# A branch for rare rows moved ahead of the last scatter, in a hard-max attention kernel

## The chip, the cores and the metric

One core of a Trainium2 chip. The time is device microseconds of the execution; before the change the median of three runs is 488.95 us (488.84 to 489.34).

## The reference

```python
def setup_inputs():
    B, Sq, Sk, D = 4, 4096, 4096, 128
    # q, k, v: standard normal, float32

def reference(q, k, v):
    logits = np.matmul(q, k.transpose(0, 2, 1))
    best = np.argmax(logits, axis=-1)
    b_idx = np.arange(q.shape[0])[:, None]
    return v[b_idx, best, :].astype(np.float32)
```

For each of 4 x 4096 query rows the kernel finds the key with the largest product and copies that key's row of v. Nothing is averaged, so a wrong winner is a wrong row.

## The kernel before, in words

The work is 128 query tiles of 128 rows (T = 128, NQT = 32 per batch). Keys are grouped by four. For each tile TensorE computes a rough fp16 score of every group, ScalarE and VectorE fold them into a packed word of score and group number, and a top-eight (line 230) leaves the best groups of every row in `TOP`. For the best group, POOL gathers the differences of its four keys (`kg`, line 247), VectorE computes the dot products and picks the winner (`pick`), and POOL gathers the winner's row of v into `vr` (line 304). Every eight tiles (four at the end) SP stores `vr` to the output (line 308). The gathers of `vr` wait in a list, `late_q`; `take_late(n)` issues the next n of them.

The order of instructions on each engine is the order in which the Python code emits them: the whole body stands in a manual schedule (`man`).

Some rows are too close to call from the rough scores. They are flagged and computed once more in fp32. The first half of the tiles is done in `flag_segment`, spread over the main loop; the second half in `flags_first` and `flags_last`, behind the main loop. `flags_last` gives up to 128 flagged rows one partition each, gathers their record, their query, and three candidate groups of keys (`FR`, `FQ`, `FK`, by the helper `get`, line 494), computes the exact products (`exact`, line 533), gathers the winners' rows of v into `FV`, and scatters `FV` to the output by the row numbers `row` (line 525). A row number beyond the output is dropped by the scatter's bounds check, which is how unused partitions are left out. Between these steps `late(n)` issues gathers of `vr`; `late(1 << 20)` ahead of the scatter issues all that are left, with their stores. As the scatter overwrites rows that the stores of `vr` have written, it must come behind them.

`HARD` counts what this way cannot settle: flags beyond 128 in a half, more than eight flagged tiles in one partition, rows whose fourth group is close too. It is the same number in all partitions, and is last changed at line 520, well ahead of the exact products. If it is above zero, `all_rows` (lines 562 to 584) computes every row again from the records in DRAM: line 564 copies the count to an integer `hi`, line 565 loads it into a register of each of the five engines' queues, line 567 branches, and the body is four loops over tiles, with stores from SP. On the inputs used here the count is zero and the branch is not taken.

When the branch is skipped, each engine's queue passes through a skip side, whose steps are put down to line 567: they bring the semaphores to where the body would have left them. On SP these are eight waits with an increment; on POOL four waits and one instruction INC_SWDGE_SEM. The end of the program is put down to line 764: SP's last waits, a DRAIN on every engine, a barrier, and the clearing of semaphores.

In the kernel before, the manual schedule ends behind `flags_last`, and `all_rows` comes after it: the scatter is issued first, then the branch.

Of the kernel before, what the change touches and what calls it, by code (L numbers as in the profile page):

```python
# [7 lines left out]
FP32 = mybir.dt.float32  # L8
FP16 = mybir.dt.float16
BF16 = mybir.dt.bfloat16  # L10
U32 = mybir.dt.uint32
# [4 lines left out]
OP = mybir.AluOpType  # L16
AF = mybir.ActivationFunctionType
IOA = bass.IndirectOffsetOnAxis
# [9 lines left out]
def kernel(ctx, tc, q, k, v, out):  # L28
    nc = tc.nc
    B, Sq, D = q.shape  # L30
    Sk = k.shape[1]
    P = 128
# [7 lines left out]
    out_flat = out.rearrange("b s d -> (b s) d")  # L40
# [7 lines left out]
    fp = ctx.enter_context(tc.tile_pool(name="flag", bufs=1))  # L48
# [82 lines left out]
    HARD = cp.tile([P, 1], FP32, tag="HARD")  # L131
# [6 lines left out]
    FV = cp.tile([P, P], FP32, tag="FV")  # L138
# [309 lines left out]
    def flags_last(t0, t1, win_last, late):  # L448
# [25 lines left out]
        for s in range(8):  # L474
# [13 lines left out]
                                op0=OP.logical_shift_right)  # L488
        nc.vector.scalar_tensor_tensor(out=rw[:, 1:2], in0=tb[:, 1:2], scalar=float(Sq - NQT), in1=rw[:, 1:2], op0=OP.mult, op1=OP.add)
        row = fp.tile([P, 1], U32, tag="row", name="row_e")  # L490
        nc.vector.scalar_tensor_tensor(out=row, in0=rw[:, 1:2], scalar=-1.0, in1=rw[:, 0:1], op0=OP.add, op1=OP.add)

        def get(dst, src, idx, hi):
# [9 lines left out]
                                op0=OP.logical_shift_right, op1=OP.logical_shift_left)  # L503
# [15 lines left out]
        for a in (hd[:, 0:1], hd[:, 1:2], tot[:, 2:3]):  # L519
# [2 lines left out]
        win = whole(exact(FK, FQ, gb, 3, "fe"))  # L522
        get(FV, v_flat, win, B * Sk)
        late(1 << 20)
        nc.gpsimd.indirect_dma_start(out=out_flat, out_offset=IOA(ap=row, axis=0), in_=FV, in_offset=None,  # L525
                                     bounds_check=P * T - 1, oob_is_err=False)

    def exact(kk, qq, grp, R, name):
        d = fp.tile([P, R, 4], FP32, tag=f"xd{R}", name=f"xd_{name}")
        for r in range(R):  # L530
            for f in range(4):
                pr = fp.tile([P, P], FP32, tag="xp", name=f"xp_{name}_{r}_{f}", bufs=2)
                nc.vector.tensor_tensor_reduce(out=pr, in0=kk[:, r, f * P:(f + 1) * P], in1=qq, scale=1.0, scalar=0.0,
                                               op0=OP.mult, op1=OP.add, accum_out=d[:, r, f:f + 1])
                yield "dve", 0.2
        ix = fp.tile([P, R, 4], FP32, tag=f"xi{R}", name=f"xi_{name}")
        nc.vector.scalar_tensor_tensor(out=ix, in0=grp.unsqueeze(2).to_broadcast([P, R, 4]), scalar=4.0,
                                       in1=iota4.unsqueeze(1).to_broadcast([P, R, 4]), op0=OP.mult, op1=OP.add)
        yield "dve", 0.17
        mx = fp.tile([P, 1], FP32, tag="xm", name=f"xm_{name}")  # L540
        nc.vector.tensor_reduce(out=mx, in_=d.rearrange("p r f -> p (r f)"), axis=AX_X, op=OP.max)
        yield "dve", 0.17
        lt = fp.tile([P, R * 4], FP32, tag=f"xl{R}", name=f"xl_{name}")
        nc.vector.tensor_scalar(out=lt, in0=d.rearrange("p r f -> p (r f)"), scalar1=mx, scalar2=float(1 << 20),
                                op0=OP.is_lt, op1=OP.mult)
        yield "dve", 0.17
        nc.vector.tensor_tensor(out=lt, in0=lt, in1=ix.rearrange("p r f -> p (r f)"), op=OP.add)
        yield "dve", 0.17
        win = fp.tile([P, 1], U32, tag="xw", name=f"xw_{name}")
        nc.vector.tensor_reduce(out=win, in_=lt, axis=AX_X, op=OP.min)  # L550
        yield "dve", 0.17
        return win


    def whole(g):
        while True:
            try:
                next(g)
            except StopIteration as s:
                return s.value  # L560

    def all_rows():
        hi = fp.tile([1, 1], mybir.dt.int32, tag="hi")
        nc.vector.tensor_copy(out=hi, in_=HARD[0:1, :])
        left = nc.values_load(hi[0:1, 0:1], min_val=0, max_val=1 << 24,  # L565
                              skip_runtime_bounds_check_because="a count of rows, summed in fp32")
        with tc.If(left > 0):
            for b in range(B):
                with tc.For_i(0, NQT, 1) as t:
                    w8 = fp.tile([P, 8], U32, tag="aw", name=f"aw_{b}")  # L570
                    nc.sync.dma_start(out=w8, in_=rec.rearrange("(p b t) w -> b p t w", b=B, t=NQT)[b][:, bass.ds(t, 1), :].rearrange("p o w -> p (o w)"))
                    qn = fp.tile([P, P], FP32, tag="aq", name=f"aq_{b}")
                    nc.sync.dma_start(out=qn, in_=q[b].rearrange("(p t) d -> p t d", p=P)[:, bass.ds(t, 1), :].rearrange("p o d -> p (o d)"))
                    g8 = fp.tile([P, 8], U32, tag="ag", name=f"ag_{b}")
                    nc.vector.tensor_scalar(out=g8, in0=w8, scalar1=NG - 1, scalar2=(NG - 1) | (b * NG),
                                            op0=OP.bitwise_and, op1=OP.bitwise_xor)
                    kk = fp.tile([P, 8, 512], FP32, tag="ak", name=f"ak_{b}")
                    for r in range(8):
                        nc.gpsimd.indirect_dma_start(out=kk[:, r, :], out_offset=None, in_=k4,
                                                     in_offset=IOA(ap=g8[:, r:r + 1], axis=0))  # L580
                    win = whole(exact(kk, qn, g8, 8, f"a{b}"))
                    vv = fp.tile([P, P], FP32, tag="av", name=f"av_{b}")
                    nc.gpsimd.indirect_dma_start(out=vv, out_offset=None, in_=v_flat, in_offset=IOA(ap=win, axis=0))
                    nc.sync.dma_start(out=out[b].rearrange("(p t) d -> p t d", p=P)[:, bass.ds(t, 1), :].rearrange("p o d -> p (o d)"), in_=vv)
# [141 lines left out]
    for p in [s for s in live if s["kind"] == "pick"]:  # L726
# [6 lines left out]
        if last:  # L733
            flags_first(T // 2, T)
        drain([p], "cnt" if last else None)
    flags_last(T // 2, T, lambda: drain([p]), take_late)
    man.__exit__(None, None, None)
    all_rows()


# [28 lines left out]
```

## Time and profile before

| what | value |
|---|---|
| median of the runs | 488.95 us |
| the profiled execution, whole | 488.95 us |
| its span, first to last instruction | 487.0 us |
| PE busy | 389.1 us, 80% |
| VectorE (DVE) busy | 421.0 us, 86% |
| ScalarE (ACT) busy | 395.5 us, 81% |
| GpSimd (POOL) busy | 302.3 us, 62% |
| last exact product's winner (`xw`, line 550) ends | 462.3 us |
| last gather of `vr` starts | 466.35 us |
| last scatter (line 525) starts | 471.86 us |

Times inside a profile are microseconds from the span's start. A name with a q (POOLq, SPq, DVEq) is the engine's instruction queue, which runs ahead of the engine and handles waits, branches, register loads and the issue of transfers; these steps are not counted as busy. A transfer's "landing" is when its semaphore says that the data are there. Durations in the answers for one line are nanoseconds.

### The profile page before, as it was taken

The page shows a single profiled execution, that of the slowest core. Times are in us where ns is not written, and L with a number is a line of the kernel's source. Part 1 is how long each engine was busy: PE and PEld are TensorE (multiplying, and loading weights), DVE is VectorE, ACT ScalarE, POOL GpSimd, SP SyncE. Part 2 cuts the span into 40 slices and gives each one's busy share as a digit, 9 for nine tenths or more (in the row PEclk, how much of TensorE's full clock was granted, in tenths as well). Part 3 has the DMA queues.
Part 4 walks back from the last instruction along what each step waited for, and adds up shares of the span by engine and source line. Part 5 has one row for each costly group of instructions (what it writes and reads, how often), then busy time and mean ns, then how long its engine had stood idle before and what let it go on. Part 6 is the DMA issues. An engine that isn't in the chain of part 4 may idle for free. (4 is left out here: it accounts for less than half of the span.)

```text
span 487.0 us, 6530 instructions
## 1 busy us (share of the span) xinstructions
PE 389.1 (80%) x1960; PEld 176.1 (36%) x1960; DVE 421.0 (86%) x849; ACT 395.5 (81%) x498; POOL 302.3 (62%) x345
## 2 busy tenths in 40 slices
PE   6798899999997999999997889999999888901000
PEld 3344444444443444444443334444433333301000
DVE  4278999999999799999998899999999999997400
ACT  1999999999997899999996889999999878900000
POOL 9025445666788676566887565576776567667730
PEclk9999999999999899999998999999999999965555
DMA  8514452131546451313456431313241311323320
GB/s 137 134 26 69 94 110 62 55 100 55 123 93 169 105 132 56 100 55 105 95 100 159 105 99 53 96 56 105 75 131 53 100 49 57 108 61 121 97 74 0
DMA packets 24552, 43.48 MB, mean 89 GB/s; under 512 B 7976, under 2 KB 16171, under 8 KB 24512
## 3 DMA queue, kind: packets, MB, share of 16 engines
q0 software_dynamic: 18464, 30.97, 28.5%
q1 hardware_dynamic: 6048, 12.06, 6.8%
q8 instruction: 15, 0.25, 0.2%
q14 instruction: 25, 0.20, 0.1%
HBM read 39.59 MB, written 12.19 MB: 106 GB/s over the span
## 5 line engine op out<-in xcount | busy, mean ns | idle before, releaser
L201 ACT ACTIVATE A<-pd 128x1024 f16<-128x1024 f32 x256 | 262.8, 1033 | 12.1 <-PE pd L192 11.6
L247 POOL DMA_INDIRECT kg<-k,cand x128 | 125.4, 979 | 121.1 <-DVE p L266 43.9
L227 DVE TENSOR_TENSOR W<-psn,E 128x1024 int16<-128x1024 f32 x128 | 166.5, 1301 | 24.1 <-ACT E L214 11.2
L192 PE MATMUL psn<-kT,qT 128*128 128x512 f16 x512 | 153.0, 380 | 18.0 <-ACT A L201 12.1
L192 PE MATMUL pd<-kT,qT 128*128 128x512 f16 x512 | 153.5, 381 | 11.1 <-ACT A L201 9.6
L230 DVE MAX8 TOP<-W 128x8 f32<-128x1024 f32 x128 | 156.2, 1220 | 0.0
L211 PE MATMUL psn<-A,identh 128*128 128x512 f16 x512 | 153.0, 380 | 0.0
L192 PEld LDWEIGHTS <-qT 128*128 128x128 f16 x1024 | 96.4, 98 | 150.0 <-issue 71.3
L304 POOL DMA_INDIRECT vr<-in_v_dram,win x128 | 124.1, 970 | 39.3 <-issue 35.6
L214 ACT ACTIVATE E<-psn 128x1024 int16<-128x1024 f32 x128 | 131.1, 1024 | 3.5 <-PE psn L211 3.5
L211 PEld LDWEIGHTS <-identh 128*128 128x128 f16 x512 | 49.9, 97 | 61.6 <-issue 1.4
L262 DVE TENSOR_TENSOR prod<-kg,natq 128x768 f16<-128x768 f16 x64 | 35.0, 549 | 0.0
L174 ACT ACTIVATE qT<-uq 128x256 f16<-128x256 f32 x60 | 23.8, 396 | 5.4 <-PE uq L172 5.4
L266 DVE TENSOR_TENSOR p<-prod 128x384 f16<-128x384 f16 x64 | 22.3, 351 | 0.0
L172 PE MATMUL uq<-identh,natq 128*128 128x128 f16 x120 | 16.6, 220 | 6.9 <-DMA natq<-in_q_dram 5.5
L271 DVE TENSOR_REDUCE D<-p 128x6 f32<-128x192 f16 x64 | 21.5, 339 | 0.0
L167 ACT ACTIVATE kT<-uk 128x256 f16<-128x256 f32 x48 | 19.0, 396 | 1.1 <-PE uk L164 1.1
L172 PEld LDWEIGHTS <-natq 128*128 128x128 f16 x120 | 11.3, 99 | 20.3 <-DMA natq<-in_q_dram 8.2
L163 PE MATMUL uk<-identh,natk 128*128 128x128 f16 x96 | 15.8, 219 | 0.6 <-ACT A L201 0.6
L63 POOL DMA_DIRECT2D natk<-in_k_dram x26 | 15.7, 602 | 0.9 <-POOLq L753 0.8
L269 DVE TENSOR_TENSOR p<-p 128x192 f16<-128x192 f16 x64 | 15.7, 248 | 0.0
L66 POOL DMA_DIRECT2D natq<-in_q_dram x26 | 15.5, 596 | 0.0
(149 smaller groups left out, 160.6 us busy)
## 6 DMA issues: line engine op xcount, KB each, us to landing
out_dram<-vr SPq DMA_DIRECT2D x14, 512.0 KB, 3.0
k<-kd SPq DMA_DIRECT2D x8, 384.0 KB, 3.3
natk<-in_k_dram POOLq DMA_DIRECT2D x24, 128.0 KB, 3.6
natq<-in_q_dram POOLq DMA_DIRECT2D x24, 128.0 KB, 3.1
kg<-k,cand POOLq DMA_INDIRECT x128, 2.7
vr<-in_v_dram,win POOLq DMA_INDIRECT x128, 2.5
natk<-in_k_dram POOLq DMA_DIRECT2D x2, 512.0 KB, 6.1
out_dram<-vr SPq DMA_DIRECT2D x4, 256.0 KB, 2.0
```

Of the source, the lines that this page charges most:

```text
L172: nc.tensor.matmul(out=ps[:, i * P:(i + 1) * P], lhsT=natq[b % 2][:, g * 2 + i, :], rhs=identh, start=True, stop=True)
L174: nc.scalar.activation(out=qT[b % 2][:, g * 256:(g + 1) * 256], in_=ps, func=AF.Copy, scale=QSCALE)
L192: nc.tensor.matmul(out=ps[:, n * 512:(n + 1) * 512], lhsT=qT[b % 2][:, qt * P:(qt + 1) * P], rhs=kT[b % 2][:, u * 1024 + n * 512:u * 1024 ...
L201: nc.scalar.activation(out=A, in_=ps, func=AF.Abs)
L211: nc.tensor.matmul(out=ps[:, n * 512:(n + 1) * 512], lhsT=identh, rhs=A[:, n * 512:(n + 1) * 512], start=False, stop=True)
L214: nc.scalar.activation(out=E, in_=ps, func=AF.Relu)
L227: nc.vector.tensor_tensor(out=W_t[t % NW].bitcast(I16)[:, 1::2], in0=ps, in1=E, op=OP.max)
L230: nc.vector.max(out=TOP[:, t, :], in_=W_t[t % NW].bitcast(FP32))
L247: near_q.append(lambda j=j: nc.gpsimd.indirect_dma_start(out=kg[:, j].rearrange("p f d -> p (f d)"), out_offset=None, in_=k16[t0 // NQT], ...
L262: nc.vector.tensor_tensor(out=prod, in0=kg, in1=natq[b % 2][:, x - b * NQT:x - b * NQT + m, :].unsqueeze(2).to_broadcast([P, m, 3, P]), op ...
L266: nc.vector.tensor_tensor(out=p1, in0=prod[:, :, :, 0:64], in1=prod[:, :, :, 64:128], op=OP.add)
L304: late_q.append(lambda j=j: nc.gpsimd.indirect_dma_start(out=vr[:, j, :], out_offset=None, in_=v_flat, in_offset=IOA(ap=win[:, j:j + 1], a ...
```

## The change

The call of `all_rows` moves from behind the manual schedule into `flags_last`, ahead of the last scatter. Since the general path would now write its rows before the scatter and not after it, the scatter must write nothing when that path has run: a mask `ok` is 2^20 in every partition when `HARD` is above a half, else zero, and is added to the row numbers, so that all of them fall beyond the output and are dropped. These are two VectorE operations on 128x1 numbers. The exact products themselves are computed as before.

```diff
         win = whole(exact(FK, FQ, gb, 3, "fe"))
         get(FV, v_flat, win, B * Sk)
         late(1 << 20)
-        nc.gpsimd.indirect_dma_start(out=out_flat, out_offset=IOA(ap=row, axis=0), in_=FV, in_offset=None,
+        ok = fp.tile([P, 1], FP32, tag="ok", name="ok_e")
+        nc.vector.tensor_scalar(out=ok, in0=HARD, scalar1=0.5, scalar2=float(1 << 20), op0=OP.is_gt, op1=OP.mult)
+        rowk = fp.tile([P, 1], U32, tag="rowk", name="rowk_e")
+        nc.vector.tensor_tensor(out=rowk, in0=row, in1=ok, op=OP.add)
+        all_rows()
+        nc.gpsimd.indirect_dma_start(out=out_flat, out_offset=IOA(ap=rowk, axis=0), in_=FV, in_offset=None,
                                      bounds_check=P * T - 1, oob_is_err=False)
...
     flags_last(T // 2, T, lambda: drain([p]), take_late)
     man.__exit__(None, None, None)
-    all_rows()
```

## The prediction

> **What bounds the kernel now.** The edit sits behind the last matrix product, so I read the end of the span first. The page's second part cuts the 487.0 us into 40 slices of 12.2 us:
>
> ```profile
> DVE  4278999999999799999998899999999999997400
> ...
> POOL 9025445666788676566887565576776567667730
> ```
>
> In the last slice no engine is busy, and in the one before it POOL has three tenths. The page's chain counts busy work and ends with POOL's last scatter, so it stops at 472.9, some 14 us before the span does. The chain of waits from 462 on:
>
> ```profile
> 466.35 0.94 POOL vr L304
> 467.30 3.66 issue
> 470.95 0.04 POOLq L525
> ...
> 472.15 0.72 POOL out_dram L525
> ```
>
> The 3.66 us called "issue" is POOL idle until its queue reaches L525 at 470.95. POOL's waits put its idle time there down to SP (total, times, longest), and SP's own timeline shows the store concerned:
>
> ```profile
> POOL out_dram L525 <- SPq L567: 4.6, 1, 4.6
> ```
>
> ```profile
> 468.88 0.33 SPq L308 DMA_DIRECT2D out_dram<-vr  x1
> ```
>
> The last store of normal rows goes out at 468.88 and lands 2.0 us later, at 470.9. The scatter writes the same output and must come behind it. Then the answer for line 567 (the branch; columns: queue, kind, count, ns min/median/max, first and last start):
>
> ```profile
> L567 SPq EVENT_SEMAPHORE  x8: 17/17/17, 470.3 to 471.3; - x8
> L567 POOLq EVENT_SEMAPHORE  x4: 17/43/1634, 472.7 to 473.0; - x4
> ...
> L567 DVEq COMPARE_BRANCH  x1: 72/72/72, 462.7 to 462.7; - x1
> L567 DVEq EVENT_SEMAPHORE  x1: 21/21/21, 465.7 to 465.7; - x1
> ...
> L567 POOLq COMPARE_BRANCH  x1: 53/53/53, 472.2 to 472.2; - x1
> L567 POOLq INC_SWDGE_SEM  x1: 2390/2390/2390, 474.6 to 474.6; - x1
> ```
>
> The body of the branch has no row in the trace: it is skipped, and these are the steps of the skip side. POOL's queue waits there until every transfer it has issued has landed; the 1.63 us wait ends at 474.6, which is the scatter's start plus its 2.7 us to landing (471.86 + 2.7). Only then comes INC_SWDGE_SEM, 2.39 us. And the kernel's last line, 764:
>
> ```profile
> L764 SPq EVENT_SEMAPHORE  x14: 17/28/28, 477.0 to 486.9; - x14
> L764 POOLq DRAIN  x3: 46/103/9056, 477.1 to 486.7; - x3
> ```
>
> One POOL DRAIN of 9.06 us begins at 477.1, straight behind INC_SWDGE_SEM, and ends at 486.1; 0.9 us of closing steps follow. So the end is a chain on POOL's queue alone: store landed 470.9, scatter 471.86, landed 474.6, INC to 477.0, DRAIN to 486.1, close at 487.0.
>
> **The change part by part.** The profiled execution took 488.95 us, which is the median of the three runs too; 1.95 us of it lies outside the span (488.95 - 487.0).
>
> The two new VectorE operations (ok, rowk) and the copy to hi, which in the trace ran at 454.4 and now stands behind them, are three 128x1 or 1x1 operations of 0.14 to 0.16 us. They run behind xw, which ends at 462.3, and are done by about 462.9. ScalarE and TensorE then load hi some 8 us later than now, and nothing else is queued on them. POOL's queue stood at L525 from 462.4 on, so it is held back by 0.5 us and still has 6 us to go until the last vr gather's landing. Cost nothing; if that cover were gone, 0.5 us.
>
> The branch moves ahead of the scatter. On POOL's queue that brings, in order: the load of hi (0.51 us), the compare, the four waits, INC_SWDGE_SEM, and then the scatter with its own waits. The load and compare are over near 463.6. A branch can cost more than its row: on VectorE 2.9 us pass from the compare at 462.7 to the next instruction at 465.7, on POOL 0.5 us (472.2 to 472.7), on SP 0.5 us (its compare at 469.8, next step at 470.3). I take POOL's own 0.5; with VectorE's 2.9 the queue would be ready at 466.5, still before the gathers have landed. [...]
>
> Now the waits of the skip side end with the last vr gather instead of the scatter: issue 466.35 plus 2.5 to landing (the median of that line's issues) is 468.85. INC_SWDGE_SEM runs from there to 471.24. Most of that lies beside the wait for the store's landing at 470.9, which the scatter has to sit out anyway. The scatter must also come behind SP's eight skip steps, the last at 471.3, because SP's stores in the body write the same output; that is a new wait, and nothing is queued behind the scatter but the end. Its four queue waits, at the 0.09 us between the two short ones of now, bring 471.65; from the queue's last wait row (ended 471.08) to the scatter's start (471.86) it was 0.78 us, so it starts at 472.43, 0.57 later than now, and ends at 473.44 with its 1.01 us.
>
> What is removed is everything now standing between the scatter's end and the DRAIN: 472.87 to 477.1, 4.2 us, that is 1.7 us of landing and 2.4 us of INC. SP's final waits still need the scatter's landing (472.43 + 2.7 = 475.1), but SP is done long before the DRAIN. DRAIN at its 9.06 us from 473.44 ends at 482.5; 0.9 to close gives a span of 483.4, and 1.95 outside it gives **485.3 us**, 3.6 below the median (0.57 lost ahead of the scatter, 4.2 gained behind it).
>
> The trace does not say what the 9.06 us are made of, nor when the DRAIN's clock starts behind a transfer in flight. The nearest rows are the opening DRAIN of POOL (0.17 us, nothing issued yet) and this one. If it takes its length from the scatter's dispatch, 1.2 us before the scatter's end, the time is 484.1; from its landing (475.1), 487.0. At the far end below, a DRAIN that only waits for the landing and adds 0.17 gives 475.3 + 0.9 + 1.95 = 478.2. At the far end above, it is paid in full twice (below). I take 9.06 from the scatter's end, as it is the same instruction behind the same list of some 320 POOL transfers. Half a microsecond either way for the queue's steps makes the likeliest case's own range 484.1 to 486.2.
>
> The main part of the kernel, up to 440, keeps its order on every engine: zero.
>
> **The rivals.** *DRAIN counts from the landing*: 487.0, faster by 1.9. For it: today it starts with everything landed, so the trace never shows it overlapping a transfer.
>
> *The 9.06 us belong to INC_SWDGE_SEM*, and DRAIN merely waits for its tail. The trace has the two back to back and cannot part them. Then the POOL engine is held from 471.24 to 480.3, the scatter starts at 481.4 and lands at 484.1, a short DRAIN of 0.17 and the close give 485.2, with 1.95 it is 487.1. Against it: SP's final waits, on the semaphores that INC raises, were released at 477.0, so INC had done its visible work by its own end.
>
> *Slower: the idle time is paid twice.* If POOL has to come to rest behind the skip side before it may issue again, and once more at the end, both at 9.06, the scatter starts at 481.4, ends at 482.4, DRAIN ends at 491.5 and the time is 494.3, 5.4 above. It decides once the second stretch is over 4.6 us (482.4 + 4.6 + 0.9 + 1.95 = 489.9). Against it: ScalarE, TensorE and VectorE run from their compare straight to line 764 without a barrier at line 567, so the skip side has no common stop, and no DRAIN row stands at line 567.
>
> *Nothing moves*: the end is tied to something that the order on POOL's queue doesn't shift, or the scatter is still issued in its old place: 488.95. Against it: the whole chain from 471.9 to 486.1 is consecutive on that one queue.
>
> *Much faster*: the DRAIN shrinks, since it no longer follows INC directly: 478.2 to 483.6.
>
> **How the numbers follow.** Likeliest case 0.62; DRAIN from the landing 0.13; INC's tail 0.07; paid twice 0.09; nothing moves 0.05; much faster 0.04. A measurement of this kernel tells about 0.2% (1.0 us) from no change. Faster: 0.62 + 0.13 + 0.07 + 0.04 = 0.86; same 0.05; slower 0.09. The range holds the likeliest case with the two that end at 487, 0.82 together, with half a microsecond of queue steps on either end: 483.6 to 487.6.
>
> **What would show it.** In the profile after, INC_SWDGE_SEM should start near 468.9 and end near 471.2, ahead of the scatter; the scatter should start at 472.1 to 472.9; DRAIN should start within 1.2 us of the scatter's end and last about 9 us; the span should be about 483.4. A gap of several us between INC_SWDGE_SEM and the scatter speaks for INC's tail or a double stop; a DRAIN of over 10 us for counting from the landing. A DRAIN row of several us at line 567, or a span above 488, makes the prediction wrong.

## The result, and the profile after

The changed kernel takes 484.63 us (median of four runs, 484.01 to 485.53) against 489.06 for the kernel before: the ratio is 0.991, with a 95% interval from 0.9891 to 0.993. The forecast was 485.3, in a range of 483.6 to 487.6. The profiled execution took 485.16 us with a span of 483.1, 3.9 below that of before.

The end of the span, first POOL's own work (start, duration, engine, line, operation):

```profile
465.99 0.95 POOL L304 DMA_INDIRECT vr<-in_v_dram,win  x1 [0.30 <-DMA vr<-in_v_dram,win]
472.18 1.01 POOL L530 DMA_INDIRECT out_dram<-FV,rowk_e  x1 [5.24 <-issue]
```

Then the answer for line 572, where the branch now stands:

```profile
L572 SPq EVENT_SEMAPHORE  x8: 17/17/17, 470.0 to 471.0; - x8
L572 POOLq EVENT_SEMAPHORE  x4: 17/43/43, 463.6 to 467.2; - x4
...
L572 POOLq COMPARE_BRANCH  x1: 53/53/53, 463.1 to 463.1; - x1
...
L572 DVEq COMPARE_BRANCH  x1: 72/72/72, 463.2 to 463.2; - x1
L572 DVEq EVENT_SEMAPHORE  x1: 21/21/21, 466.2 to 466.2; - x1
L572 POOLq INC_SWDGE_SEM  x1: 2370/2370/2370, 468.6 to 468.6; - x1
```

and for line 768, the end of the program:

```profile
L768 SPq EVENT_SEMAPHORE  x14: 17/28/3199, 471.1 to 483.0; - x14
...
L768 POOLq DRAIN  x3: 46/109/10311, 471.9 to 482.8; - x3
```

INC_SWDGE_SEM has changed sides: it runs from 468.6 to 470.9, behind the landing of the last gather and ahead of the scatter. The scatter starts 0.3 us later than before, at 472.18, and ends at 473.2. The long DRAIN row begins when POOL's queue reaches it, at 471.9, even ahead of the scatter; it ends at 482.3, which is 9.07 us behind the scatter's end. Nothing stands between the two any more. The scatter lands at 474.4 (SP's 3.2 us wait in line 768 ends there) while the DRAIN runs.

### The profile page after: what moved, and what is told of

It is laid out like the page before. It is cut to its first block, busy times and chain, and to the rows that moved or that the text cites. A ratio compares the mean times of both kernels' runs of the same rounds, so it can differ in the third digit from the quotient of the medians.

```text
span 483.1 us, 6533 instructions
## 1 busy us (share of the span) xinstructions
PE 389.5 (81%) x1960; PEld 176.5 (37%) x1960; DVE 419.8 (87%) x851; ACT 395.4 (82%) x498; POOL 303.4 (63%) x345
## 4 chain that ended last, share of the span: by engine, by line
DVE 39%; ACT 21%; issue 17%; PE 11%; DMA 7%; POOL 3%; POOLq 0%; DVEq 0%; ACTq 0%
ACT A L201 16%; DVE W L227 16%; DVE TOP L230 7%; DMA natq<-in_q_dram 4%; ACT E L214 4%; DVE prod L262 4%; PE psn L192 4%; PE pd L192 3%; PE psn L211 3%; DVE p L266 2%; DVE D L271 2%; DMA vr<-in_v_dram,win 2%; POOL vr L304 1%; DVE cand L241 1%; DVE p L269 1%
## 5 line engine op out<-in xcount | busy, mean ns | idle before, releaser
L201 ACT ACTIVATE A<-pd 128x1024 f16<-128x1024 f32 x256 | 262.5, 1031 | 11.5 <-PE pd L192 11.0
L172 PE MATMUL uq<-identh,natq 128*128 128x128 f16 x120 | 16.6, 220 | 7.3 <-DMA natq<-in_q_dram 5.8
```

Source lines behind the costliest of these rows:

```text
L172: nc.tensor.matmul(out=ps[:, i * P:(i + 1) * P], lhsT=natq[b % 2][:, g * 2 + i, :], rhs=identh, start=True, stop=True)
L201: nc.scalar.activation(out=A, in_=ps, func=AF.Abs)
```

## The experiments

The loop's length differs a little from run to run, so the table gives, besides the ratio to the kernel before of the same set, the length of the end alone: from the start of the last gather of v (line 304) to the end of the span, all from the profiled executions.

| kernel | ratio to before (95%) | scatter after last gather, us | INC_SWDGE_SEM, us | DRAIN's end after the scatter's end, us | length of the end, us |
|---|---|---|---|---|---|
| before | 1 | 5.5 | 2.39 | 13.3 | 20.6 |
| mask_only | 1.0017 (0.9999 to 1.0035) | 5.6 | 2.39 | 13.2 | 20.6 |
| after | 0.991 (0.9891 to 0.993) | 6.2 | 2.37 | 9.07 | 17.1 |
| after_again | 0.9906 (0.9878 to 0.9934) | 6.3 | 2.37 | 9.07 | 17.2 |
| move_only | 0.992 (0.9868 to 0.9971) | 6.1 | 2.37 | 9.07 | 17.0 |
| no_branch | 0.988 (0.9852 to 0.9907) | 5.5 | none | 9.06 | 16.3 |
| branch_early | 1.0016 (0.9993 to 1.0039) | 5.6 | 2.31 | 9.07 | 16.6 |
| extra_12 | 0.9776 (0.9753 to 0.9799) | 6.0 | 0.50 | 1.99 | 9.9 |
| extra_30 | 0.9801 (0.9773 to 0.9829) | 6.3 | 0.86 | 2.86 | 11.0 |
| before_12 | 0.9816 (0.9749 to 0.9882) | 5.6 | 0.52 | 4.2 | 11.6 |

move_only and before_12 ran together on a chip on which the kernel before takes 519.8 us; their loops are some 23 to 33 us longer (by the start of the last top-eight), so only the ratio and the end are used of them. In branch_early INC_SWDGE_SEM runs ahead of the last gather, so its cost does not show in the last column.

**The parts of the change.** The mask without the move, and the move without the mask, both as edits of the changed kernel:

```diff
 # mask_only: the branch stays behind the scatter
         nc.vector.tensor_tensor(out=rowk, in0=row, in1=ok, op=OP.add)
-        all_rows()
...
     man.__exit__(None, None, None)
+    all_rows()
 # move_only
-        nc.gpsimd.indirect_dma_start(out=out_flat, out_offset=IOA(ap=rowk, axis=0), in_=FV, in_offset=None,
+        nc.gpsimd.indirect_dma_start(out=out_flat, out_offset=IOA(ap=row, axis=0), in_=FV, in_offset=None,
```

> The kernel before with the mask alone: ok and rowk are computed and the scatter uses rowk, but the branch stays behind it. Theory: the two operations lie on VectorE behind xw, 9 us ahead of the scatter, and cost nothing: 489, as before, with the scatter near 471.9 and INC_SWDGE_SEM behind its landing. Rival, the gain is the mask's, or the operations hold POOL: 1 us or more from 489.

> The changed kernel with row in place of rowk in the scatter: the branch is moved, the mask is left out of use (if the general path were taken, the scatter would overwrite its rows). Theory: all of the gain is the move's: 484.5 to 485.3, the scatter at 472.2, the closing DRAIN 9.07 us from its end. Rival, part of it comes with the mask: over 486.

mask_only is 489.29 us, ratio 1.0017, and its end is that of before to 0.1 us. move_only's ratio is 0.992 and its end that of after to 0.1 us. The count `HARD` is zero in all of these runs, so neither the mask's other value nor the general path ran in any of them. The gain is the move's alone; the absolute times expected of move_only were not met, as the chip was another.

**The changed kernel once more**, as the measure of its set:

> The changed kernel as it is, so that the others of this set stand beside it on the same chip. Expected 484 to 485.5 us, against 489 before.

It is 484.96 us.

**Whose are the 9 us?** The kernel before, without the general path:

```diff
     man.__exit__(None, None, None)
-    all_rows()
```

> The kernel before without the general path: no load of hi, no branch, no skip side (rows that need it would stay as the scatter leaves them). It parts INC_SWDGE_SEM from the closing DRAIN. Theory A, the DRAIN's 9.07 us are its own and count from the scatter's end: scatter at 471.9 to 472.9 as before, DRAIN ends at 482.0, span 482.8, time 484.7, the same as the changed kernel, because there INC_SWDGE_SEM lies beside the wait for the last store. Theory B, the 9 us are INC_SWDGE_SEM's tail: the DRAIN ends soon after the scatter's landing at 474.6, span about 475.5, time about 477.5.

It takes 484.41 us. The scatter in the answer for its line, and the DRAIN in the answer for the last line:

```profile
L525 POOL DMA_INDIRECT out_dram<-FV,row_e x1: 1019/1019/1019, 472.1 to 472.1; - x1
```

```profile
L763 POOLq DRAIN  x3: 46/97/10310, 471.9 to 482.7; - x3
```

With no INC_SWDGE_SEM near it the DRAIN still ends 9.06 us behind the scatter's end (471.9 + 10.31 = 482.2, less 472.1 + 1.02). Theory A holds, and the tail of INC_SWDGE_SEM is no explanation. The run also prices what is left of the branch in the changed kernel: the scatter comes 5.5 us after the last gather here and 6.2 there, so SP's and POOL's skip steps still cost 0.7 us.

**Is the skip side free only under its cover?** The branch ahead of the last three gathers:

```diff
-        late(1 << 20)
         ok = fp.tile([P, 1], FP32, tag="ok", name="ok_e")
...
         all_rows()
+        late(1 << 20)
         nc.gpsimd.indirect_dma_start(out=out_flat, out_offset=IOA(ap=rowk, axis=0), in_=FV, in_offset=None,
```

> The changed kernel with the branch one step earlier still: ahead of the last three gathers of v, and so without the cover of the wait for the last store (the general path's rows of the last tiles would be overwritten, were it taken). Theory A, the skip side is free only because it lies beside that wait: INC_SWDGE_SEM then runs from the landing of FV, about 465.0, to 467.4, the three gathers follow at 1.25 us each and land at about 473, the last store lands at 475.1, the scatter starts at 476.0, the DRAIN ends at 486.1, time 488.9, some 4 us above the changed kernel. Rival, the skip side costs nothing wherever it stands: 485.

The median is 490.05 us and the profiled execution 488.93. POOL's timeline:

```profile
461.29 1.00 POOL L494 DMA_INDIRECT FV<-in_v_dram,xw_fe  x1 [1.17 <-DVE hi L569]
467.81 0.94 POOL L304 DMA_INDIRECT vr<-in_v_dram,win  x1 [5.52 <-DMA FK<-in_k_dram,gb_e]
...
475.93 1.02 POOL L530 DMA_INDIRECT out_dram<-FV,rowk_e  x1 [4.68 <-issue]
```

POOL stands still for 5.5 us between FV and the next gather: the wait for the landing, then INC_SWDGE_SEM (464.8 to 467.1), then the restart. The scatter starts at 475.93, where 476.0 was expected. One step too early costs all that the change gains.

**What does the closing DRAIN count?** A DRAIN was put into POOL's order in the loop, behind iterations 30, 60, 90 and 118 (drain_4), behind 64 (drain_1), behind every eighth (drain_8), and, in drain_qe, behind iterations without loads, with one more ahead of the branch:

```diff
         step(it)
         issue(it)
+        if it in (30, 60, 90, 118):        # drain_1: (64,)   drain_8: it % 8 == 6
+            nc.gpsimd.drain()
...
+        nc.gpsimd.drain()                  # drain_qe only
         all_rows()
```

> The changed kernel with a DRAIN put into POOL's order behind iterations 30, 60, 90 and 118 of the main loop. It asks what the closing DRAIN's length counts. Theory C, it counts the transfers issued on POOL since the last DRAIN (about 322 now, so 28 ns each): some 50 are left after iteration 118, the closing DRAIN takes about 1.4 us from the scatter's end or ends with the scatter's landing, and the span is 6 to 8 us shorter at its end; each DRAIN in the loop holds POOL for some 2.5 us of landing and 2 us of its own, of which VectorE may wait 0 to 3 us; time 478 to 484. Theory D, it has a fixed length, or one that goes with the whole program: it stays at 9 us, the loop pays as well, time 485 to 520.

drain_4 takes 492.65 us, ratio 1.0073 (1.0047 to 1.0098): the time falls in theory D's range, but not with theory D's DRAIN. Its closing DRAIN and scatter:

```profile
L770 POOLq DRAIN  x3: 46/109/5139, 484.5 to 490.2; - x3
```

```profile
484.71 1.01 POOL L530 DMA_INDIRECT out_dram<-FV,rowk_e  x1 [4.93 <-SPq L572]
```

484.5 + 5.14 = 489.6, which is 3.9 us behind the scatter's end instead of 9.07. So the length does go with the transfers since the last DRAIN, but not at 28 ns: counted in the trace, the five DRAINs have 61, 76, 76, 62 and 47 POOL transfers behind them and end 5.06, 6.27, 6.26, 5.12 and 3.90 us after the last of them, 82 to 83 ns for each. At that price 9.07 us are 111 transfers, where 322 were issued. drain_4's end is 11.6 us long, 5.5 shorter than that of after, but its last top-eight starts 11.6 us later: the loop pays more than the end gains.

> The changed kernel with one DRAIN on POOL, behind iteration 64. From the run with four, each DRAIN took 82 ns for every POOL transfer issued since the last one (3.90 us for 48, 5.06 for 59, 6.27 for 76, from the last transfer's end), but the closing DRAIN of the changed kernel takes 9.07 for 322, which at 82 ns are 111 transfers. Theory E, the count has a ceiling of about 110: both DRAINs here have more behind them (about 165 and 155), so both take about 9 us from the last transfer's end. Theory F, the price per transfer falls with their number (28 ns at 322): the closing DRAIN has half the transfers and takes 4.5 to 7 us.

One run, 485.69 us. The DRAIN behind iteration 64, and the transfer just ahead of it:

```profile
L702 POOLq DRAIN  x1: 5809/5809/5809, 223.6 to 223.6; - x1
```

```profile
225.16 0.99 POOL L304 DMA_INDIRECT vr<-in_v_dram,win  x1 [0.30 <-issue]
```

It ends at 229.4, 3.29 us behind that transfer's end: 40 transfers' worth, where 145 had been issued. The closing DRAIN and the scatter:

```profile
L770 POOLq DRAIN  x3: 46/109/7113, 475.6 to 483.3; - x3
```

```profile
475.84 1.02 POOL L530 DMA_INDIRECT out_dram<-FV,rowk_e  x1 [5.00 <-SPq L572]
```

This DRAIN ends 5.87 us behind the scatter's end: 71 transfers' worth of 177. Theory E, a ceiling with 9 us for both, is wrong. The closing length lies in theory F's span, but F can't explain why 145 transfers cost 3.29 and 177 cost 5.87. What comes near all three numbers is an estimate worked out from them alone: that the length stands for the transfers since the last DRAIN less about 106, once or more often: 145 - 106 = 39, 177 - 106 = 71, 322 - 2 x 106 = 110. The step back can't come at every 106 sharp, for then the 322 would have met a third one at 318 and left 4, where 9.07 us are 111 transfers' worth. Theory G below pictures this as a list that is emptied on its own. That is the author's guess at the cause: the traces show the lengths, and no row of a list or of its emptying.

The estimate was put to the test by adding transfers rather than DRAINs, 12 or 30 of 4 KB on POOL's queue, into a tile that nobody reads:

```diff
+    SCR = cp.tile([P, 8], FP32, tag="SCR", name="SCR")
...
         step(it)
         issue(it)
+        if it < T - NQT and it % NQT in (20, 22, 24, 26):     # extra_30: 19 to 28
+            nc.gpsimd.dma_start(out=SCR, in_=q_flat[0:P, 0:8])
```

> The changed kernel with 12 more transfers on POOL, 4 KB each into a tile that nobody reads, four in each of the first three batches in iterations without other loads. The run with one DRAIN fits neither a ceiling nor a falling price: at 82 ns its two DRAINs had 40 of 145 and 71 of 177 transfers to count, and the closing DRAIN of the changed kernel 111 of 322. All three fit a list that is emptied on its own about every 106 transfers (145 - 106 = 39, 177 - 106 = 71, 322 - 2 x 106 = 110). Theory G, that is so: the third emptying would come just behind the present end, the 12 more push it into the program, and the closing DRAIN counts 5 to 20, under 2 us from the scatter's end; the loop hides the 12 transfers (0.6 us each of POOL's idle time); time 477 to 479. Theory H, nothing is emptied at such a step: the DRAIN counts 123, 10.0 us, time 485.5 to 486.5.

> The same with 30 more transfers, ten in each of the first three batches. Theory G: the closing DRAIN counts 25 to 35, 2.1 to 2.9 us from the scatter's end, INC_SWDGE_SEM takes about 0.8 us; time 478 to 481. Theory H: it counts 141, 11.5 us, time 487 to 489. If the list has room for more than 120, the first of the two runs shows a longer DRAIN and this one a short one.

extra_12 takes 477.03 us (475.9 to 479.3) against 488.11 for the kernel before, and extra_30 479.15. In extra_12:

```profile
465.56 0.95 POOL L305 DMA_INDIRECT vr<-in_v_dram,win  x1 [0.30 <-issue]
471.55 1.02 POOL L531 DMA_INDIRECT out_dram<-FV,rowk_e  x1 [5.05 <-SPq L573]
```

```profile
L573 POOLq INC_SWDGE_SEM  x1: 500/500/500, 468.4 to 468.4; - x1
```

```profile
L771 POOLq DRAIN  x3: 46/109/3236, 471.3 to 475.2; - x3
```

The DRAIN ends 1.99 us behind the scatter. In extra_30:

```profile
L771 POOLq DRAIN  x3: 46/109/4107, 471.9 to 476.5; - x3
```

```profile
472.08 1.02 POOL L531 DMA_INDIRECT out_dram<-FV,rowk_e  x1 [5.36 <-SPq L573]
```

Here it ends 2.86 us behind the scatter (35 transfers' worth at 82 ns). More transfers make the end 6.1 to 7.2 us shorter: theory G foretold both numbers, theory H would have had 10.0 and 11.5. The lengths of INC_SWDGE_SEM step back in the same place: 2.31 us in branch_early with 318 transfers issued ahead of it, 2.37 in after with 321, but 0.50 in extra_12 with 333. So, by the estimate, the third step comes behind 321 transfers and at the latest at 333. That something is emptied there was not seen.

**DRAINs in the loop as a remedy.**

> The changed kernel with a DRAIN on POOL behind every eighth iteration (6, 14, ... 118, 126). By 82 ns for each transfer since the last one, every DRAIN in the loop takes some 1.6 us plus the last landing, which POOL's idle time in the loop may hide (in the run with four DRAINs, the 5.06 us of the first one cost the loop 0.1 us); about 44 transfers are left for the closing DRAIN, 3.6 us from the scatter's end. Theory: the end is 5.4 us shorter, the loop 0 to 3 us longer, time 479 to 483. Rival, the loads at the batches' changes wait for the DRAINs, as the jump of 4.5 us near iteration 45 in that run hints: loop 5 us or more longer, time 485 to 492.

> The changed kernel with DRAINs on POOL only in those iterations of a batch in which no loads for the next batch are issued (19, 23, 27, 31 of each of the first three batches, then every sixth), and one more ahead of the branch, behind the last gather of v. Theory: the loop's DRAINs hide, 0 to 1.5 us on the loop; the DRAIN ahead of the branch ends some 3.6 us behind the last gather's landing (468.5), at about 472.1, INC_SWDGE_SEM finds nothing left and takes under 0.3 us, the scatter starts near 473.5, and the closing DRAIN ends with its landing, about 475.8 to 476.2; time 478.5 to 481. Rival, as above: the loop loses what the end gains, 484 to 490.

drain_8 takes 491.05 us, as the rival had it. drain_qe takes 496.39, 6 us above even the rival's range: its direction is right, its size is not. drain_8's end is 10.2 us long and its loop 8.2 us longer than that of after. Where it went, in TensorE's waits between 100 and 470 us (line waiting, releaser, total, times, longest), drain_8:

```profile
PE uq L172 <- DMA natq<-in_q_dram: 13.2, 2, 7.0
```

and after:

```profile
PE uq L172 <- DMA natq<-in_q_dram: 5.8, 2, 3.2
```

The queries of the next batch are loaded by POOL's queue, and TensorE waits for them at two changes of batch, 7.4 us longer in drain_8 than in after, where the whole loop is 8.2 longer. The DRAINs push these loads back: the first of them goes out at 155.6 instead of 152.2 at one change, at 262.9 instead of 253.6 at the next. drain_qe, which kept its DRAINs out of the iterations with loads, lost 14 us in the loop, so that keeping clear of the loads' own iterations is not enough. There TensorE waits longer for the same loads, and for those of the keys as well, for which it does not wait in after:

```profile
PE uq L172 <- DMA natq<-in_q_dram: 10.1, 2, 5.1
PE uk L163 <- DMA natk<-in_k_dram: 3.8, 2, 2.1
```

That is 8.1 us more than in after; where the rest of the 14 went is open. The closing DRAIN of drain_qe has a single transfer between it and the DRAIN before and ends 1.28 us behind it, and its INC_SWDGE_SEM takes 0.19 us, as expected.

**The change's worth where the DRAIN is short.** The kernel before, with the 12 transfers of extra_12:

> The kernel before with the 12 more transfers of the run extra_12, so that the change is priced where INC_SWDGE_SEM is short (0.50 us there, not 2.4) and the closing DRAIN too. Theory: what the change removes is the scatter's landing (1.7 us) and INC_SWDGE_SEM, whatever its length, less the 0.2 to 0.6 us by which the scatter comes later; here that is about 1.7 us. Scatter near 471.9, landed 474.6, INC to 475.1, DRAIN about 1 us shorter than the 1.99 of extra_12 because the scatter has already landed, time 478.0 to 480, that is 1 to 2.5 us above extra_12. Rival, the 9 us at the end belong to the old order: time 485 or more.

Its ratio is 0.9816 (0.9749 to 0.9882), which at 489 us would be 480.0. The time expected was not met as such, on that chip. In the ends, which the chip hardly touches (17.0 us in move_only on this chip, 17.1 in after), it is 11.6 us against 9.9 for extra_12: 1.7 us, as expected, instead of 3.5 between before and after. INC_SWDGE_SEM takes 0.52 us there, and the DRAIN, whose transfers have all landed, 1.38, where about 1.0 was expected:

```profile
L568 POOLq INC_SWDGE_SEM  x1: 520/520/520, 503.2 to 503.2; - x1
```

## Why the prediction was right

*INC_SWDGE_SEM changes sides.* Forecast from 468.85 to 471.24; measured from 468.56 to 470.93. The last gather started 0.36 us earlier than in before, so against it INC_SWDGE_SEM came 0.07 late.

*The scatter comes a little later.* Forecast 0.57 us later, at 472.43; measured at 472.18, or against the last gather 0.68 later than in before. SP's last skip step at 471.0 and the end of INC_SWDGE_SEM at 470.9 hold it together, as the sum had them. no_branch confirms the size: without the branch 0.7 us of this go.

*Nothing left between the scatter and the DRAIN.* Forecast 4.2 us removed. Measured: the DRAIN's end lies 13.25 us behind the scatter's end in before and 9.07 in after, 4.2 less. With the 0.68 this is 3.5 us on the end of the span, where the prediction had 3.6.

*The DRAIN counts from the scatter's end at 9.06.* This was the choice with the widest bounds, and it held to 0.01 us in five kernels. The reason given, the same list of some 320 transfers, was only half of it: at 82 ns for each, the length is that of about 111, and the traces show no list. The choice held, as far as these runs go, because the change leaves the number of POOL's transfers at 322; it did not rest on knowing what the length counts, and to that extent it was luck: with 12 transfers more the same reasoning would have been 7 us out (extra_12). Had it been counted from the landing, the DRAIN would have ended at 483.5 (474.4 + 9.07) and not at 482.3. One of the signs named was badly chosen: a DRAIN row of over 10 us was to speak for the landing, but the row begins when the queue reaches the instruction, 0.23 us ahead of the scatter, and so is 10.31 long in the likeliest case too.

*Terms that were off without effect.* POOL's load of `hi` took 0.81 us and not 0.51, but under cover; the scatter landed 2.2 us after its start and not 2.7, but only SP waits for that, and the DRAIN ends later; outside the span lay 2.05 us in the profiled execution and not 1.95.

*The rivals.* The tail of INC_SWDGE_SEM is ruled out by no_branch, the double stop by the scatter's start at 472.18, "nothing moves" by the ratio. The much shorter DRAIN is possible on this kernel, but not through this change: extra_12 has it (1.99 us).

*The time behind the compare.* VectorE again needs 3.0 us from its compare (463.2) to the next step (466.2), POOL 0.5 (463.1 to 463.6), as the prediction took it. VectorE's 3.0 us are off the path; what they are, no run shows.

*The remainder.* 485.3 was forecast from an end 3.6 us shorter; the median came out 4.4 us below that of before, the profiled execution 3.8, of which 0.35 are a loop that ended earlier. The rest was not traced to a row; the loop's last top-eight comes at 432.6 in after, 432.9 in before and 431.8 in after_again, so that much lies within what the loop varies by.

## What to carry to other kernels

Read what stands behind the last busy instruction: here the last 14 us were queue steps without a row in the chain of work, and the 3.5 us that the change gains lay in them. In these runs the skip side, on which POOL's queue waits for the landing of its last transfer (468.5 in after) and then runs INC_SWDGE_SEM, was nearly free (0.7 us) where the next step waits for a landing anyway, and cost all of the gain one place earlier (branch_early, 490.05 us) or later (before, 489.06). A fixed-looking cost at the end may be a count: the DRAIN's 9.07 us were 3.90 in drain_4 and 1.99 in extra_12. Vary the count before accepting it.

## What the runs showed of the hardware

In drain_4 POOL's five DRAINs, with 47 to 76 transfers since the one before, ended 3.90 to 6.27 us behind the last transfer's end, 82 to 83 ns for each. In drain_qe's loop, with 8 transfers, they ended 1.9 to 2.1 us behind the last; its closing one, with a single transfer, 1.28. From 145 transfers on the length came to less than 82 ns for each, and it was shorter again from 322 to 334: 3.29 us at 145 and 5.87 at 177 (drain_1), 9.07 at 322 (after), 1.99 at 334 (extra_12), 2.86 at 352 (extra_30). The steps of about 106 transfers are an estimate from these lengths; what the length counts, and why and where it steps back, no run shows.

INC_SWDGE_SEM on the skip side was longer where the DRAIN of the same run was longer: 2.37 us in after (DRAIN of 111 transfers' worth), 1.59 in drain_1 (71), 1.12 in drain_4 (47), 0.86 in extra_30 (35), 0.19 in drain_qe, just behind a DRAIN. That is close to 0.2 us and 20 ns for each transfer of the DRAIN's worth, an estimate from these five lengths.

The best kernel of the set is extra_12, ratio 0.9776 against 0.991 for the changed kernel. That is with 334 transfers on POOL's queue; with 352 (extra_30) the ratio is 0.9801, with 322 (after) 0.991, and what another number gives was not run.
